# Spreading the sample's cross-attention scores over more of the prompt's work, and giving its projections two banks

## The chip, the cores and the metric

The kernel runs on one core of one Trainium2 chip. The metric is the device time of one execution in microseconds (us). Before the change three runs took 1911.37, 1909.26 and 1916.39 us; their median is 1911.37 us. Five engines work side by side: TensorE (PE, matrix products; its weight loads are listed apart as PEld), VectorE (DVE), ScalarE (ACT), GpSimd (POOL, here mostly an issuer of transfers) and SyncE (SP, an issuer of transfers). Each takes its own instructions strictly in their order, and waits on semaphores for the others.

## The reference

One step of a small decoder with a single layer. It is computed for two groups that share all weights: a prompt of 1024 tokens, and a "sample" of 8 sequences that each add one token to a memory of 8192 cached tokens. Width is 1024, all arithmetic float32.

```python
xp = xp + merge_heads(fox_prompt(q, k, v, logf), sgu_prompt(u, z, ...), ..., w_o)
xp = xp + cross_attend(rmsnorm(xp, g_cross), mk, mv, w_cq, w_co)
xp = xp + conv_ffn(rmsnorm(xp, g_ffn), 0, w_up, conv_w, conv_b, w_down)

att = fox_sample(q, k, v, logf, cache_k, cache_v, cache_logf, page_table)
xs = xs + merge_heads(att, sgu_sample(u, z, ...), ..., w_o)
xs = xs + cross_attend(rmsnorm(xs, g_cross), cache_mem_k, cache_mem_v, w_cq, w_co)
xs = xs + conv_ffn(rmsnorm(xs, g_ffn), state_conv, w_up, conv_w, conv_b, w_down)

def cross_attend(xn, mk, mv, w_cq, w_co):
    q = (xn @ w_cq).reshape(B, T, MEM_HEADS, MEM_HEAD_DIM)
    s = jnp.einsum('bqhd,bmhd->bhqm', q, mk) * (MEM_HEAD_DIM ** -0.5)
    p = jax.nn.softmax(s, axis=-1)
    o = jnp.einsum('bhqm,bmhd->bqhd', p, mv).reshape(B, T, MEM_HEADS * MEM_HEAD_DIM)
    return o @ w_co
```

The change touches the sample's line with `cross_attend` and the projection by `w_o` ahead of it. Here T is 1, there are 4 heads of 256, and each of the 8 sequences has its own cached memory of 256 tokens (1 MB of keys and 1 MB of values each). After both groups are through, each is normalised once more and written out.

## The kernel before

**Two streams of work.** The prompt is written as one Python generator, `prompt()`: projections, attention and the rest in two halves of 512 tokens (`hf` 0 and 1). The sample is another, `sample()`: first the attention over the paged memory (`decode`), then `sample_rest`, which holds everything from the merge of heads to the final output. Both emit instructions into one program. The loop at the end of `build` runs the prompt's generator; each of its yields names an estimate of the microseconds just emitted, which is added to `acc`. Whenever `acc` has reached `PACE` of the running phase (2.9 for `sample_rest`), one step of the sample's generator is drawn and `PACE` taken off:

```python
while bgs and not held[0] and most and acc[0] >= PACE[phase[1] or phase[0]]:
    most -= 1
    acc[0] -= PACE[phase[1] or phase[0]]
    if next(bgs[0], None) is None:
        bgs.pop()
```

So the number of yields in a piece of the sample's code sets how densely it is mixed into the prompt. A scheduler with a model of the engines' times then settles the order of the instructions on each engine; `behind(e)` (L1249) tells it to place what is emitted under it after the newest instruction of the prompt on engine e. The order that counts is therefore that of the built program. In the stretch in question the prompt is in the feed-forward part (`ffn`, L1159) of its second half.

**The prompt's feed-forward.** 22 pairs of columns of `w_up` are taken in groups of 6, 6, 5 and 5. For each of a group's pairs there are two "up" tiles. A tile loads 512 KB of `w_up` by SyncE (L223), splits it into a rounded part on ACT (L209, `wh`) and a remainder on DVE (L210, `wl`), and runs 24 matmuls (L246 to L248) into one bank of PSUM. The bank is read by ACT (L1192, L1193) and then by two DVE operations of the convolution (L1194, L1195); a small one, L1197, mends the first two columns. Per pair follow a SiLU on ACT (L1200), a product on DVE (L1201) and a split into two `u` buffers (ACT L209, DVE L210). After a group's up tiles come its "down" tiles: two halves of columns, each with splits of `w_down` (L209, L210), four row tiles of matmuls, and an addition on DVE (L1226). The prompt's banks are four `ba` and two `bb`; a tile cannot start before its bank's last reader is done. Raw weights have 4 buffers, `wh` 5, `wl` 4.

**The sample's part.** It has two banks of its own, `ms` and `dv`, four buffers `kv` of 1 MB and five `d2` buffers. `sample_proj` multiplies the 8 rows by a 1024x1024 weight (`w_o`, `w_cq` and `w_co` in turn): for each half n of the columns it loads two `kv` buffers by POOL (L1474), runs 8 matmuls (L258) into bank `ms`, copies the bank to a `d2` buffer on ACT (L1462), and folds the four partial sums by one more matmul, again into `ms` (L1465). The second half's matmuls cannot start before the first half's fold has been read. For `w_cq` the result is scaled on DVE (L1520) and written to memory, `q2s_d`, by SyncE (L1521).

The scores follow (L1526 to L1537). For each of the 8 sequences POOL loads the two halves of its query, spread over all partitions (L1529, two `d2` buffers), and its 1 MB of cached keys (L1531, one `kv` buffer); DVE multiplies (L1535, two products of 128x1024) and sums over each head's 256 columns (L1536, one reduce of 128x2048). One yield follows each sequence. Then come the transposes (L1541), a softmax, the cached values (L1564, L1568), the `w_co` projection and the sample's own feed-forward (L1610 to L1653).

Of the kernel before, what the change touches and what calls it, by code (L numbers as in the profile page):

```python
# [12 lines left out]
ALU = mybir.AluOpType  # L13
AX = mybir.AxisListType
PSUM = bass.MemoryType.PSUM
ENG = mybir.EngineType
DRAM = bass.MemoryType.DRAM

P = 128
# [10 lines left out]
FF = 2816  # L30
NF = FF // P
NPAGE = 64
EPS = 1e-6
NEG = -1e30
UW = 1024
# [40 lines left out]
PACE = {'p1': 7.0, 'att0': 20.0, 'mid0': 8.0, 'ffn0': 8.5, 'att1': 15.0, 'mid1': 6.8, 'ffn1': 2.5, 'rest': 2.9}  # L76


def build(nc, tc, ctx, a, phases=None):
# [13 lines left out]
    def nm(s):  # L93
        cnt[0] += 1
        return f"{s}_{cnt[0]}"
# [13 lines left out]
    def KV():  # L109
        return dpool.tile([P, 2048], F32, tag="kv", bufs=NKV, name=nm("kv"))  # L110

    def sm(shape, tag, bufs=2, dt=F32):
        return small.tile(shape, dt, tag=tag, bufs=bufs, name=nm(tag))
# [4 lines left out]
    def BB():  # L118
        return psum.tile([P, 512], F32, tag="bb", bufs=2 + MB, name=nm("bb"))
# [9 lines left out]
    def MS():  # L129
        return BB() if MB else psum.tile([P, 512], F32, tag="ms", bufs=1, name=nm("ms"))  # L130

    def DV():
        return psum.tile([P, 512], F32, tag="dv", bufs=1, name=nm("dv"))

    def D2(n=512, dt=F32):
        return dpool.tile([P, 512], dt, tag="d2", bufs=5, name=nm("d2"))[:, :n]
# [25 lines left out]
    epsb = const.tile([P, 1], F32, tag="epsb", name="epsb")  # L162
    nc.vector.memset(epsb, EPS)
    warm = const.tile([P, 1], F32, tag="warm", name="warm")
# [28 lines left out]
    def rstd_of(ssq, n, width, tag):  # L193

        p = ssq.shape[0]
        r = sm([P, width], tag + "r", 2)[:p]
        nc.vector.tensor_scalar(r, ssq, 1.0 / n, EPS, op0=ALU.mult, op1=ALU.add)
        nc.gpsimd.tensor_tensor(r, r, mhalf[:p, :width], op=ALU.pow)
# [54 lines left out]
    def sample_mm(ps, raw, kk, xT, n, off=0):  # L253

        for q in range(2):
            k = kk * 2 + q
            j = k % 4
            mmul(  # L258
                ps[32 * j : 32 * j + 32, :n],
                xT[:, k, :],  # L260
                raw[:, q, off : off + n],
                start=(k < 4),
                stop=(k >= 4),
                tile_position=(0, 32 * j),
            )
# [43 lines left out]
    def p1(early):  # L309
# [25 lines left out]
        def stats(hf):  # L335
# [9 lines left out]
            for dst, m in ((rstd8, 64.0), (rstd, 1.0)):  # L345
                v = sm([P, 4], "xv", 2)
                nc.vector.tensor_scalar(v, ssx[:, c], m / D, m * EPS, op0=ALU.mult, op1=ALU.add)
                nc.gpsimd.tensor_tensor(dst[:, c], v, mhalf[:, :4], op=ALU.pow)
# [898 lines left out]
    bgs, acc, phase = [], [0.0], ["p1", None]  # L1247

    def behind(e):  # L1249

        return tc.issue_after(last[e]) if e in last else nullcontext()
# [208 lines left out]
    def sample_out(n, ps, fin):  # L1460
        t = D2()
        nc.scalar.activation(t, ps, AF.Copy)  # L1462
        yield 1
        ps2 = MS()
        mmul(ps2[:8, :], selS, t, start=True, stop=True)  # L1465
        fin(n, ps2[:8, :])

    def sample_proj(w, xT, fin):
        for n in range(2):
            ps = MS()  # L1470
            for kk in range(4):
                if kk % 2 == 0:
                    raw = KV().rearrange("p (k n) -> p k n", n=512)
                    nc.gpsimd.dma_start(raw, w[kk * 256 : (kk + 2) * 256, n * 512 : (n + 1) * 512].rearrange("(k p) n -> p k n", p=P))  # L1474
                    yield 1
                sample_mm(ps, raw[:, (kk % 2) * 2 : (kk % 2) * 2 + 2, :], kk, xT, 512)
            yield from sample_out(n, ps, fin)

    def sample_rest(xs):
        yield 1  # L1480
# [31 lines left out]
        def add(n, ps):  # L1512
            nc.vector.tensor_tensor(xs[n], ps, xs[n], op=ALU.add)

        yield from sample_proj(a["w_o"], xsT, add)
        yield from sample_norm(xs, gp[:, G_CROSS : G_CROSS + 8], xsT)
        q2s = pair("s")

        def toq(n, ps):
            nc.vector.tensor_scalar(q2s[n], ps, 1.0 / 16, None, op0=ALU.mult)  # L1520
            nc.sync.dma_start(q2s_d[:, n * 512 : (n + 1) * 512], q2s[n])  # L1521

        yield from sample_proj(a["w_cq"], xsT, toq)

        sS = sm([P, 2, 8, 4], "sS", 1)
        for b in range(8):  # L1526
            qb = [D2(), D2()]
            for n in range(2):
                nc.gpsimd.dma_start(qb[n], q2s_d[b : b + 1, n * 512 : (n + 1) * 512].broadcast_to((P, 512)))  # L1529
            kv = KV()  # L1530
            nc.gpsimd.dma_start(kv.rearrange("p (a c) -> p a c", c=D), a["cmk"][b].rearrange("(a p) c -> p a c", p=P))  # L1531
            kvv = kv.rearrange("p (a c) -> p a c", c=D)
            for n in range(2):
                kn = kvv[:, :, n * 512 : (n + 1) * 512]
                nc.vector.tensor_tensor(kn, kn, qb[n].unsqueeze(1).broadcast_to((P, 2, 512)), op=ALU.mult)  # L1535
            nc.vector.tensor_reduce(sS[:, :, b, :], kv.rearrange("p (a h d) -> p a h d", a=2, h=4), axis=AX.X, op=ALU.add)  # L1536
            yield 1  # L1537
        yield 1
        tr = MS()
        for mt in range(2):  # L1540
# [21 lines left out]
        for b in range(8):  # L1562
            kv = KV().rearrange("p (a c) -> p a c", c=D)
# [11 lines left out]
            op=ALU.mult,  # L1575
# [3 lines left out]
        for n in range(2):  # L1579
            ps = MS()  # L1580
# [3 lines left out]
        sample_T(y, ones[:, 0:8], xsT)  # L1584
        yield 1
        yield from sample_proj(a["w_co"], xsT, add)
        yield from sample_norm(xs, gp[:, G_FFN : G_FFN + 8], xsT)

# [14 lines left out]
        for f4 in range(11):  # L1603
            ps = DV()
# [60 lines left out]
        for n in range(2):  # L1665
            ps = (DV, MS)[n]()
# [89 lines left out]
    def sample():  # L1756
        yield from decode()
        phase[1] = "rest"
        yield from sample_rest(pair("dec"))
# [4 lines left out]
    for t in prompt():  # L1764
        ins = nc.cur_bb.bb.instructions
        for e in (ENG.DVE, ENG.PE):
            for i in range(len(ins) - 1, max(seen, len(ins) - 400) - 1, -1):
                if ins[i].engine == e:
                    last[e] = ins[i]
                    break  # L1770
        acc[0] += t
        most = int(t / PACE[phase[1] or phase[0]]) + 1
        while bgs and not held[0] and most and acc[0] >= PACE[phase[1] or phase[0]]:
            most -= 1
            acc[0] -= PACE[phase[1] or phase[0]]
            if next(bgs[0], None) is None:
                bgs.pop()
        seen = len(nc.cur_bb.bb.instructions)
    for _ in bgs.pop() if bgs else ():
        pass  # L1780
# [90 lines left out]
```

## Time and profile before

| what | value |
|---|---|
| median of three runs | 1911.37 us |
| the profiled execution | 1913.18 us |
| its span, first to last instruction | 1911.4 us |
| mean granted TensorE clock | 0.978 |
| PE busy | 1816.1 us, 95% |
| DVE busy | 1404.6 us, 73% |
| ACT, POOL busy | 761.7 us (40%), 480.6 us (25%) |
| score products L1535 | 16, 1216 ns each, from 1583.8 to 1636.3 us |
| score reduces L1536 | 8, 2274 ns each, from 1593.3 to 1643.4 us |

The profile is one execution. A page gives the busy time of each engine, the chain of work that ended last, and the costliest groups of instructions by line and shape; `ba<-wh,u` reads "written bank, then what was read". Further views of the same trace give the waits of an engine (who waited, for what, how often and how long), windows (the busy time of every engine in a stretch, the granted clock, the DMA engines' share and rate), and the timeline, where each line is one instruction with its start, its length and, in brackets, the idle time ahead of it and what ended that. Matmuls overlap: an instruction is listed as 0.39 us long, but a new one starts every 0.23 us while the clock is full. "Start to start" below is that second kind of time.

### The profile page before, as it was taken

Reading aid. Unit: us, or ns where it says so; the run is one execution under the profiler, and the core shown is the slowest. Engines: PE = TensorE matmul, PEld = TensorE weight load, DVE = VectorE, ACT = ScalarE, POOL = GpSimd, SP = SyncE. Lnnn points to the kernel's source line nnn. Section 1 sums busy time; section 2 is a strip of 40 time slices with the busy share of each in tenths; the row PEclk is TensorE's granted clock in tenths of the full one; section 3 lists DMA queues with packets and bytes.
Section 4 is the critical chain, followed back from the end, with each engine's and each line's share of the span. In section 5 each row is a group of like instructions: output and inputs, shape, how many; then the busy total and the mean of one; then the engine's idle time right before and its main releaser. Section 6 shows DMA issues by size and latency. Waiting matters only on the chain.

```text
span 1911.4 us, 24216 instructions
## 1 busy us (share of the span) xinstructions
PE 1816.1 (95%) x9255; PEld 1296.3 (68%) x9255; DVE 1404.6 (73%) x1662; ACT 761.7 (40%) x1435; POOL 480.6 (25%) x429
## 2 busy tenths in 40 slices
PE   8999999778898999999999999998999999899998
PEld 5987666555676667777777776775665667667765
DVE  4888678777777887989989998887864548754344
ACT  5332356566633435333333244324353333232232
POOL 1232342222121332213432322354222012101110
PEclk9999999989998999999999999998999999899999
DMA  8777988743395876759878879888859557676872
GB/s 322 286 245 278 323 319 302 265 162 119 128 399 210 324 268 256 297 206 359 313 264 313 301 304 344 340 338 302 307 206 362 191 200 265 215 242 247 320 280 101
DMA packets 156373, 517.07 MB, mean 271 GB/s; under 512 B 20169, under 2 KB 41929, under 8 KB 123489
## 3 DMA queue, kind: packets, MB, share of 16 engines
q0 software_dynamic: 56400, 339.04, 47.7%
q1 hardware_dynamic: 92944, 163.89, 24.7%
q10 hardware_dynamic: 6912, 12.59, 1.7%
q8 instruction: 73, 1.20, 0.2%
q14 instruction: 44, 0.35, 0.1%
HBM read 493.63 MB, written 21.84 MB: 270 GB/s over the span
## 4 chain that ended last, share of the span: by engine, by line
PE 66%; DVE 8%; ACT 3%; DMA 3%; issue 2%; POOL 0%; SPq 0%; DVEq 0%; POOLq 0%; ACTq 0%
PE ba L247 9%; PE ba L246 9%; PE ba L248 9%; PE bb L246 6%; PE bb L247 5%; PE bb L248 5%; PE dv L1371 5%; DMA kv<-cache_k,kidx 2%; DVE kv L1312 1%; DVE s L1316 1%; PE dv L1614 1%; PE ba L973 1%; PE ba L975 1%; PE ba L974 1%; PE bb L772 1%
## 5 line engine op out<-in xcount | busy, mean ns | idle before, releaser
L209 ACT ACTIVATE wh<-wr 128x1024 fp32r<-128x1024 f32 (+2 forms) x220 | 228.8, 1044 | 488.8 <-PE ba L247 147.8
L210 DVE TENSOR_TENSOR wl<-wr,wh 128x1024 fp32r<-128x1024 f32 (+2 forms) x220 | 262.5, 1200 | 166.7 <-PE ba L248 71.3
L1306 POOL DMA_INDIRECT kv<-cache_k,kidx x128 | 179.8, 1405 | 545.6 <-DVE s L1316 249.3
L1312 DVE TENSOR_TENSOR kv<-kv,d 128x2048 f32<-128x2048 f32 (+1 forms) x139 | 292.3, 2113 | 28.2 <-DMA kv<-cache_k,kidx 26.9
L1316 DVE TENSOR_REDUCE s<-kv 128x32 f32<-128x2048 f32 (+1 forms) x139 | 292.0, 2106 | 0.6
L1365 POOL DMA_INDIRECT kv<-cache_v,kidx x128 | 181.3, 1416 | 424.2 <-PE dv L1371 169.6
L246 PE MATMUL ba<-wh,u 128*128 128x512 f32 (+1 forms) x596 | 226.9, 382 | 0.0
L247 PE MATMUL ba<-wl,u 128*128 128x512 f32 (+1 forms) x596 | 226.2, 380 | 0.0
L248 PE MATMUL ba<-wh,u 128*128 128x512 f32 (+1 forms) x596 | 223.4, 380 | 1.0 <-DVE u L210 1.0
L246 PE MATMUL ba<-u,wh 128*128 128x512 f32 (+2 forms) x520 | 203.0, 391 | 1.3 <-DVE u L213 1.2
L247 PE MATMUL ba<-u,wh 128*128 128x512 f32 (+2 forms) x520 | 203.8, 392 | 0.0
L248 PE MATMUL ba<-u,wl 128*128 128x512 f32 (+2 forms) x520 | 202.7, 390 | 0.0
L1371 PE MATMUL dv<-kv,s 128*32 128x512 f32 x1024 | 138.0, 618 | 6.8 <-DMA kv<-cache_v,kidx 6.8
L246 PE MATMUL bb<-u,wh 128*128 128x512 f32 (+2 forms) x344 | 138.2, 402 | 1.8 <-DVE u L213 1.8
L247 PE MATMUL bb<-u,wh 128*128 128x512 f32 (+2 forms) x344 | 136.5, 397 | 2.5 <-DVE u L213 2.5
L248 PE MATMUL bb<-u,wl 128*128 128x512 f32 (+2 forms) x344 | 135.9, 396 | 0.0
L246 PEld LDWEIGHTS ba<-wh,u 128*128 128x128 f32 x596 | 112.7, 189 | 31.4 <-issue 8.0
L248 PEld LDWEIGHTS ba<-wh,u 128*128 128x128 f32 x596 | 112.1, 189 | 29.0 <-issue 6.3
L247 PEld LDWEIGHTS ba<-wl,u 128*128 128x128 f32 x596 | 112.4, 189 | 23.8 <-issue 2.9
L247 PEld LDWEIGHTS ba<-u,wh 128*128 128x128 f32 x520 | 98.7, 190 | 33.3 <-issue 13.0
L246 PEld LDWEIGHTS ba<-u,wh 128*128 128x128 f32 x520 | 98.5, 190 | 31.7 <-issue 7.1
L248 PEld LDWEIGHTS ba<-u,wl 128*128 128x128 f32 x520 | 98.5, 189 | 28.5 <-issue 9.3
(418 smaller groups left out, 3105.5 us busy)
## 6 DMA issues: line engine op xcount, KB each, us to landing
wr<-w_up SPq DMA_DIRECT2D x88, 512.0 KB
kv<-w_up POOLq DMA_DIRECT2D x22, 1024.0 KB
wr<-w_down SPq DMA_DIRECT2D x40, 512.0 KB
kv<-w_down POOLq DMA_DIRECT2D x11, 1024.0 KB
wr<-w_in SPq DMA_DIRECT2D x16, 512.0 KB
wr<-w_o SPq DMA_DIRECT2D x16, 512.0 KB
wr<-w_cq SPq DMA_DIRECT2D x16, 512.0 KB
wr<-w_co SPq DMA_DIRECT2D x16, 512.0 KB
```

Source lines behind the costliest of these rows:

```text
L209: nc.scalar.activation(h, src, AF.Copy)
L210: nc.vector.tensor_tensor(l, src, h.bitcast(F32), op=ALU.subtract)
L246: mmul(out, sh, mh, start=(i == 0), stop=False)
L247: mmul(out, sh, ml, start=False, stop=False)
L248: mmul(out, sl, mh, start=False, stop=(i == n - 1))
L772: mmul(po[64 * j : 64 * j + 64, q0:256], vn[:, kt, 64 * j : 64 * j + 64], pt[j][kt // 4][:, kt % 4, q0:256], start=(kt == 0), stop=(kt == ...
L973: mmul(pss[i], mh[k][:, tb], wh, start=(k == korder[0]), stop=False)
L1306: nc.gpsimd.indirect_dma_start(kv, None, a["cache_k"], off(kidx[:, b, ch : ch + 1]))
L1312: nc.vector.tensor_tensor(kvv[:, i : i + m, :], kvv[:, i : i + m, :], qb.unsqueeze(1).broadcast_to((P, m, 512)), op=ALU.mult)
L1316: nc.vector.tensor_reduce(s[:, ch * 4 + i : ch * 4 + i + m, :].rearrange("p k h -> p (k h)"), kvv[:, i : i + m, :].rearrange("p k (h d) -> ...
L1365: nc.gpsimd.indirect_dma_start(kv, None, a["cache_v"], off(kidx[:, b, ch : ch + 1]))
L1371: mmul(dv[32 * j : 32 * j + 32, :], s[:, ch * 4 : ch * 4 + 4, :].rearrange("p k h -> p (k h)"), kvv[:, j, :], start=(ch == 0), stop=(ch == ...
```

## The change

Three things are edited.

1. In the score loop each sequence now yields `CMK` = 3 instead of 1, and the driving loop takes w times `PACE` from `acc` for a step that yields w. A sequence's scores thus use up three steps of the prompt's time instead of one.
2. The score operations are emitted under `behind(ENG.DVE)`, and the one reduce of 128x2048 becomes two of 128x1024. DVE has 8 instructions more in all.
3. In `sample_proj` the first half's sums and fold go to bank `dv`, the second's to `ms`. Both halves' matmuls are issued before either fold. A projection has 5 yields instead of 6.

PE, ACT, POOL and SP issue as many instructions as before.

```diff
+CMK = 3
@@ sample_out
-        ps2 = MS()
+        ps2 = (DV, MS)[n]()
         mmul(ps2[:8, :], selS, t, start=True, stop=True)
         fin(n, ps2[:8, :])
@@ sample_proj
+        outs = []
         for n in range(2):
-            ps = MS()
+            ps = (DV, MS)[n]()
             for kk in range(4):
                 if kk % 2 == 0:
                     raw = KV().rearrange("p (k n) -> p k n", n=512)
                     nc.gpsimd.dma_start(raw, w[...])
                     yield 1
                 sample_mm(ps, raw[:, (kk % 2) * 2 : (kk % 2) * 2 + 2, :], kk, xT, 512)
-            yield from sample_out(n, ps, fin)
+            outs.append(sample_out(n, ps, fin))
+            next(outs[n])
+        for o in outs:
+            yield from o
+        yield 1
@@ sample_rest, for b in range(8)
-            for n in range(2):
-                kn = kvv[:, :, n * 512 : (n + 1) * 512]
-                nc.vector.tensor_tensor(kn, kn, qb[n]..., op=ALU.mult)
-            nc.vector.tensor_reduce(sS[:, :, b, :], kv.rearrange("p (a h d) -> p a h d", a=2, h=4), axis=AX.X, op=ALU.add)
-            yield 1
+            with behind(ENG.DVE):
+                for n in range(2):
+                    kn = kvv[:, :, n * 512 : (n + 1) * 512]
+                    nc.vector.tensor_tensor(kn, kn, qb[n]..., op=ALU.mult)
+                for i in range(2):
+                    nc.vector.tensor_reduce(sS[:, i, b, :], kvv[:, i, :].rearrange("p (h d) -> p h d", h=4), axis=AX.X, op=ALU.add)
+            yield CMK
@@ the driving loop
-            if next(bgs[0], None) is None:
+            w = next(bgs[0], None)
+            if w is None:
                 bgs.pop()
+            else:
+                acc[0] -= (w - 1) * PACE[phase[1] or phase[0]]
```

## The prediction

> **What bounds the kernel now.** I read the page first, then the waits of TensorE, then windows of 20 us, then single instructions.
>
> ```profile
> PE 1816.1 (95%) x9255; PEld 1296.3 (68%) x9255; DVE 1404.6 (73%) x1662; ACT 761.7 (40%) x1435; POOL 480.6 (25%) x429
> PE 66%; DVE 8%; ACT 3%; DMA 3%; issue 2%; POOL 0%; SPq 0%; DVEq 0%; POOLq 0%; ACTq 0%
> ```
>
> TensorE (PE) is the bound, so a change is worth what it adds to or takes from PE's own stream or its idle time. Up to about 1521 us both programs issue the same instructions in the same order on every engine; the first that differs is the sample's w_o block. In the 390 us behind it PE waits twice, and the windows (columns: PE, PE weight loads, DVE, ACT, POOL busy; then the granted clock) show where:
>
> ```profile
> PE bb L246 <- DVE t L1197: 8.0, 1, 8.0
> PE ba L248 <- DVE u L210: 1.0, 1, 1.0
> ...
> 1540.00:1560.00 20.00, 20.00 (x98) 13.90 (x96) 12.36 (x19) 9.29 (x13) 1.06 (x2) 1.00 0.54 200
> 1560.00:1580.00 20.00, 20.00 (x92) 13.12 (x89) 9.92 (x15) 8.35 (x14) 2.95 (x5) 1.00 0.70 247
> 1580.00:1600.00 20.00, 20.00 (x88) 16.35 (x88) 13.76 (x16) 6.00 (x10) 4.99 (x9) 1.00 0.67 193
> 1600.00:1620.00 20.00, 20.00 (x89) 16.26 (x88) 20.00 (x21) 7.36 (x13) 5.42 (x9) 1.00 0.84 303
> 1620.00:1640.00 20.00, 12.01 (x42) 8.97 (x40) 20.00 (x22) 3.92 (x5) 1.99 (x3) 0.74 0.67 230
> ```
>
> VectorE (DVE) is full from 1592 to 1648 us, half empty before. The timeline (start, length, instruction, idle before) shows PE without a bank:
>
> ```profile
> 1621.61 0.40 PE L248 MATMUL ba<-wh,u 128*128 128x512 f32 x1
> 1630.00 0.77 PE L246 MATMUL bb<-wh,u 128*128 128x512 f32 x1 [7.99 <-DVE t L1197]
> 1630.57 0.63 PE L247 MATMUL bb<-wl,u 128*128 128x512 f32 x1
> ```
>
> and, on DVE, why: the bank's last reader, L1195 at 1629.12, stood behind score work.
>
> ```profile
> 1620.59 2.35 DVE L1535 TENSOR_TENSOR kv<-kv,d 128x1024 f32<-128x1024 f32 x2
> 1622.86 2.28 DVE L1536 TENSOR_REDUCE sS<-kv 128x8 f32<-128x2048 f32 x1
> 1625.06 1.21 DVE L210 TENSOR_TENSOR wl<-wr,wh 128x1024 fp32r<-128x1024 f32 x1
> 1626.19 1.22 DVE L1535 TENSOR_TENSOR kv<-kv,d 128x1024 f32<-128x1024 f32 x1
> 1629.12 0.73 DVE L1195 SCALAR_TENSOR_TENSOR t<-bb,gp,t 128x510 f32<-128x510 f32 x1
> ```
>
> From start to start PE loses 8.39 - 0.23 = 8.2 us (its step is 0.23). The clock row is 0.5 from 1624.46 to 1634.70, so the 11 matmuls from 1630.00 step by 0.43: 11 x 0.20 = 2.2 us. A wait at 1641.09 costs 1.1 (step 1.38), smaller ones 0.5. Together 12.0 us, what the scores cost PE today.
>
> **The change part by part.** *Score work.* Per sample row b: two products and a reduce. Start to start a product takes 1.13 us (two in 2.27, above), the reduce 2.20. Split in two it costs two reduces of half size; L1316 has that shape, 1207 ns long, 1.13 start to start, so 2.26. Eight rows: 8 x (2.27 + 2.26) = 36.2 us against 35.8. The added 0.4 us lies on DVE, not on PE.
>
> *Where it goes.* Before, the scores start on DVE at 1583.8 and share eight up tiles. After, the projections end earlier (next part) and the rows come every 3 x 2.9 / 5.2 = 1.7 tiles (yields times PACE, over a tile's own estimate) instead of every 0.6. In the changed DVE order the first product stands behind the first read of up tile 2 of 12, and 12 products and 12 half reduces stand ahead of the L1195 that came late. I sum the order from the first product to that L1195: 12 x 1.13 + 12 x 1.13 (scores) + 9 x 1.13 (weight splits, L210) + 8 x 0.66 (L1194) + 8 x 0.66 (L1195) + 8 x 0.07 (L1197) + 3 x 0.60 (L1201) + 2 x 0.61 (split of u) = 51.4 us.
>
> *When it starts (T1).* By matmul counts, w_cq's block runs at 1544 to 1547.8 and its folds end at 1551.2 and 1554.6. SyncE writes q2s at 1555.4. Before, the second write went out at 1580.99, its load was issued at 1585.42 and DVE started at 1589.47: 8.5 us. So T1 is 1564 at best. At worst the load queues behind the four cmk loads (4 MB), now issued ahead of it on POOL's queue: before, the first q2s load, behind 2 MB, took from 1574.68 to 1583.67, 9.1 us; doubled, 18 us, T1 = 1578. But the 4 MB go out at 1546 to 1549, 11 us or more ahead of the load (before it was 1.6 us), and this queue alone moves about 1 MB in 2.5 us from 3 us after the issue (the DMA view's best slices stand at 399 GB/s), so they are in at 1560 to 1563. I take T1 = 1565.
>
> *What it does to PE.* 1565 + 51.4 = 1616.4 against 1620.5, when PE needs that bank: the 8.2 and 2.2 us go. Late next are the splits of u and the copies for the first down tiles: the same sum carried on gives 1628.9 against 1628.5 and 1630 against 1629.5. The last reduce ends at 1634 to 1637 (before 1645.7). I charge 0.5 to 1.5 us here, take 1.0, and each us of T1 beyond 1565 costs one more. The gain cannot exceed the 12.0.
>
> By the Trainium skill, page "TensorE: Matmul & The Clock Gate", Part 1 on the HAM clock gate, the clock halves after one idle window of about 3.4 us. The trace agrees, with a halved clock in an 8.0 us wait; by that rule a rest under 3.4 us costs only itself, so the sum stays; without it the row's 2.2 per 8.2 us would make 1.0 into 1.3.
>
> *Two banks.* Three projections each trade two blocks of 8 sample matmuls for one of 16. Eight cost PE 2.04 us of its stream (1520.81 to 1523.31 less one step), the block of 16 at L1568 3.76: 2 x 2.04 - 3.76 = 0.3 us, three times 0.9. Folds stay six. The price: the block needs both halves of the weights. w_cq's four loads now all go out at 1522.5 to 1525.3 (buffers come free with w_o's single block) and at 2.5 us per MB plus 3 are in by 1538, needed at 1544. w_co's have 30 us more. Lower bound 0, upper bound 5 us each; taken 0, since the queue's row fits.
>
> *Queues.* SyncE: both q2s writes move ahead of the w_up loads of tiles 9 on. The first load behind them went out at 1557.4 before, the second write now at 1555.4: nothing lost. POOL: cmk loads wait for w_cq's block, not each for a half; same order otherwise. The product held behind the prompt's last DVE instruction (`behind`) waits with prompt reads behind it: L1195 of tile 2, then the weight splits. That is covered while T1 stays near 1565. ACT's copies keep 2.3 us and more to the fold (before 5.0); a copy takes 0.60.
>
> Sum: -12.0 + 1.0 - 0.9 = -11.9. The profiled execution took 1913.2 us (span 1911.4, 1.8 around it), 1.8 above the median of 1911.4. 1913.2 - 11.9 = 1901.3, or 1899.5 against the median; I say 1900.5.
>
> **Rivals.** *B, the backlog only shrinks.* T1 at 1568 to 1573, or the boundary to the down tiles stalls by as much for another reason: a rest of 4 to 9 us, plus 2.2 of half clock, 1904 to 1911. For it: at the boundary my sum leaves nothing over. Against: at 1616 there are 4 us, and T1 has its own 2 us of margin behind the four cmk loads.
>
> *C, slower: DVE's head blocks.* If q2s lands late, the first product holds L1195 and the splits behind it. The loss is T1's lateness plus 1.0, plus 2.2 of half clock. From about 10 us late (T1 1575) that is more than the 12.0 and the 0.9 saved now; 19 us late (T1 1584, where the first product stood before) it is 22.2, 10 us more than now: 1921. For it: DVE already waited for q2s three times:
>
> ```profile
>   DMA d<-q2s_d: 6.2, 3
> ```
>
> Against: the 4 MB lead by 11 us. The Trainium skill, page "DMA: Bandwidth & Descriptors", section "Queues, rings and completion order", says, of the queues that SyncE and ScalarE issue on, that each DMA engine consumes descriptors in ring order; if POOL's queue is alike, small loads pass nothing. That speaks against this change; the 9.1 us behind 2 MB agree. Worked from those rows alone, the whole 4 MB unmoved at the issue gives T1 1578, a loss of 16.2 and 1915: the near end of C, which needs another 6 us.
>
> *D, PE waits in the merged blocks,* for loads or for the copy before a fold: 1 to 6 us, 1901 to 1907.
>
> *E, nothing moves.* The transposes that end the scores stand at the same place of PE's order, two matmuls apart; were the first product to start at 1580 again at the old density, the 12.0 would stay: 1910 to 1912. The changed order speaks against it.
>
> **How the numbers follow.** Forecast 0.62 (1897 to 1903), B 0.14 (0.02 of it far worse than its range), D 0.10, C 0.12 (1915 and more, 0.09 of it beyond 1921), E 0.02. The forecast is the likeliest, so 1900.5. The range leaves out C, E and 0.05 of thin tails: 1896 to 1911. A measurement tells about 0.5%, 9.6 us, from no change: faster means below 1901.8. Of the forecast 0.56 and of D 0.04 lie there: 0.60. Slower, beyond 1921, takes 0.09 of C and those 0.02 of B: 0.11. The rest is 0.29.
>
> **What would show it.** Right: no PE wait over 3 us after 1521, clock 1.0 through 1640, the first score product near 1565 and the last reduce before 1638; DVE at 15 to 18 of 20 us from 1560 to 1620; three blocks of 16 sample matmuls without a gap. Wrong: DVE idle before the first product with a q2s load as what ends it (C, or B), a PE wait on L209 or L210 at the first down tiles (B), on a kv load or L1462 at the blocks (D), or a stall like today's at the same bank (E).

## The result, and the profile after

The changed kernel takes 1902.57 us (median of 20 runs, 1896.12 to 1912.05) against 1911.33 us (20 runs) before: the ratio is 0.9952, with a 95% interval from 0.9942 to 0.9962. That is 9.2 us less by the ratio, a little under the 9.6 us that I had called tellable, though with 20 runs each the interval lies clear of 1; 1900.5 was forecast. The profiled execution took 1900.45 us, its span 1898.7 us.

The waits of TensorE behind the w_o block, and the same windows as before (PE, PE weight loads, DVE, ACT, POOL; then the granted clock). In the changed file the lines up to the projections stand one further down, the scores are L1542 and L1544:

```profile
PE ms L284 <- DVE s L1456: 1.1, 1, 1.1
```

```profile
1540.00:1560.00 20.00, 20.00 (x98) 12.21 (x98) 8.41 (x10) 8.46 (x11) 5.18 (x9) 1.00 0.91 333
1560.00:1580.00 20.00, 20.00 (x88) 16.30 (x87) 19.55 (x23) 6.87 (x13) 5.09 (x9) 1.00 0.83 248
1580.00:1600.00 20.00, 20.00 (x88) 16.32 (x88) 20.00 (x25) 8.31 (x14) 3.79 (x7) 1.00 0.90 304
1600.00:1620.00 20.00, 20.00 (x89) 16.30 (x88) 20.00 (x28) 7.56 (x13) 1.86 (x3) 1.00 0.66 222
1620.00:1640.00 20.00, 20.00 (x89) 15.69 (x88) 17.32 (x25) 6.72 (x9) 1.43 (x2) 1.00 0.57 187
```

PE is busy through all five windows and its clock is full: the 8.0 us wait and the halved clock are gone. DVE is full from 1561 instead of from 1592 us, and has slack again from 1630. Its timeline at the start of the scores (start, length, instruction) shows no idle time ahead of the first product, and prompt work between the products:

```profile
1560.38 0.75 DVE L1195 SCALAR_TENSOR_TENSOR t<-ba,gp,t 128x511 f32<-128x511 f32 x1 [0.36 <-ACT hlast L1194]
1561.18 1.23 DVE L1542 TENSOR_TENSOR kv<-kv,d 128x1024 f32<-128x1024 f32 x1
1562.32 0.74 DVE L1196 SCALAR_TENSOR_TENSOR t<-ba,gp,t 128x510 f32<-128x510 f32 x1
1562.98 0.15 DVE L1198 TENSOR_TENSOR t<-t,fix 128x2 f32<-128x2 f32 x1
1563.17 0.69 DVE L1202 TENSOR_TENSOR t<-t,t 128x512 f32<-128x512 f32 x1
1563.78 1.22 DVE L1542 TENSOR_TENSOR kv<-kv,d 128x1024 f32<-128x1024 f32 x1
```

Two executions differ by some 3 us before either program reaches the change: the last prompt matmul ahead of the w_o block starts at 1520.81 us before and at 1517.70 after, in the same order of work. So I measure each profile from the start of the first matmul of that w_o block (L258 of before) to the start of PE's last instruction, and call it the stretch. Before it is 382.7 us, after 372.8: 9.9 less. A second profile of the changed kernel (below) has 370.9.

Of the 12.0 us lost before, none is left up to the end of the scores. But 2.8 us have come up later, at a place that I had not looked at. The first two lines are PE's timeline, the others POOL's; in brackets is the idle time ahead and what ended it:

```profile
1715.10 0.81 PE L284 MATMUL ms<-cp,s 8*128 8x8 f32 x8 [1.10 <-DVE s L1456]
1716.90 0.63 PE L249 MATMUL ba<-u,wl 128*128 128x512 f32 x1
```

```profile
1696.44 1.57 POOL L1618 DMA_DIRECT2D kv<-w_up  x2 [0.16 <-issue]
1713.25 0.72 POOL L1618 DMA_DIRECT2D kv<-w_up  x1 [15.23 <-DMA o_s<-kv]
1713.99 0.55 POOL L199 TENSOR_TENSOR r1r<-r1r,mhalf 8x1 f32<-8x1 f32 x1
```

The transposes of the sample's third norm (L284) wait for the normalised row, that for the power that makes the norm (L199, on POOL), and that stands in POOL's queue behind a load of the sample's w_up. The load waits 15.2 us for its buffer, which a store of the convolution's state (`o_s1`, in 5632 pieces of 8 numbers) still reads. That store was issued at 1697.3 and had company: from 1702 to 1706 us only 376 packets of under 512 bytes went through while POOL's queue moved 1.62 MB (the loads ahead), from 1706 to 1710, with 0.42 MB left to move, 5184. From start to start PE loses 1.25 us there, and then eight matmuls at 0.43 instead of 0.23, 1.5 us. Before, the same four w_up loads stood in the same order on POOL, but three of them could not go out before w_co's second block:

```profile
1711.31 0.70 POOL L1610 DMA_DIRECT2D kv<-w_up  x1 [25.68 <-PE ms L258]
1724.06 2.28 POOL L1610 DMA_DIRECT2D kv<-w_up  x3 [12.04 <-PE ms L258]
1733.84 0.55 POOL L198 TENSOR_TENSOR r1r<-r1r,mhalf 8x1 f32<-8x1 f32 x1 [7.50 <-DVE r1r L197]
```

There the store (issued at 1713.2) lay beside that wait, with one load ahead of it instead of three: 5018 small packets went from 1717 to 1721. No load waited for it, and the power waited for its own input only. So the earlier loads met the store and, by these counts, also made it slower; no run separates the two.

### The profile page after: what moved, and what is told of

Same layout as the page of the kernel before. It is cut to its first block, busy times and chain, and to the rows that moved or that the text cites. A ratio compares the mean times of both kernels' runs of the same rounds, so it can differ in the third digit from the quotient of the medians.

```text
span 1898.7 us, 24235 instructions
## 1 busy us (share of the span) xinstructions
PE 1810.4 (95%) x9255; PEld 1295.8 (68%) x9255; DVE 1404.6 (74%) x1670; ACT 760.9 (40%) x1435; POOL 475.4 (25%) x429
## 4 chain that ended last, share of the span: by engine, by line
PE 83%; DVE 6%; ACT 4%; DMA 4%; issue 2%; POOL 0%; SPq 0%; DVEq 0%; POOLq 0%; ACTq 0%
PE ba L247 12%; PE ba L248 12%; PE ba L249 12%; PE bb L247 7%; PE bb L248 7%; PE bb L249 7%; PE dv L1372 6%; DVE kv L1313 2%; DMA kv<-cache_k,kidx 2%; DVE s L1317 1%; PE dv L1622 1%; PE ba L974 1%; PE ba L976 1%; PE ba L975 1%; PE ms L773 1%
## 5 line engine op out<-in xcount | busy, mean ns | idle before, releaser
L1307 POOL DMA_INDIRECT kv<-cache_k,kidx x128 | 175.8, 1373 | 552.4 <-DVE s L1317 252.9
```

The costliest lines, as they stand in the source:

```text
L1307: nc.gpsimd.indirect_dma_start(kv, None, a["cache_k"], off(kidx[:, b, ch : ch + 1]))
```

## The experiments

Theory and rivals: the stall went because the scores start earlier (the projections' part), because they are less dense (the scores' part), or only by both. For the new wait: POOL's queue, or the norm's own chain.

**The changed kernel again, either part alone, and the changed kernel with the store out of the way.** These four ran on one chip, in five rounds beside the kernel before (1909.8 us there).

The changed kernel, not edited:

> The changed kernel itself, once more, as the measure for the others beside it. Both theories: 8 to 11 us faster than the kernel before (ratio 0.994 to 0.996), no TensorE wait over 3 us after the w_o block, one wait of about 1 us at the transposes of the sample's third norm (L284) with a stretch of half clock of about 3.4 us behind it.

Measured: 1901.53 us, ratio 0.9958 (0.9945 to 0.9971); the stretch is 370.9 us. The one wait is at L284, 0.7 us, and here the clock stays full behind it, so the half-clock part of the expectation was not met: its 1.5 us stands in one of the two profiles.

The projections alone: `CMK`, `behind`, the halved reduce and the loop's charge are taken back.

```diff
-            with behind(ENG.DVE):
-                ...
-            yield CMK
+            for n in range(2):
+                kn = kvv[:, :, n * 512 : (n + 1) * 512]
+                nc.vector.tensor_tensor(kn, kn, qb[n]..., op=ALU.mult)
+            nc.vector.tensor_reduce(sS[:, :, b, :], ...)
+            yield 1
```

> The two-bank projections alone: the scores keep one yield per sequence, the one reduce of 128x2048, and are not held behind the prompt's DVE work. Theory 'start' (the stall went because the projections end earlier and the first score product moves from 1583.8 to about 1561 us): the 36 us of score work begins 22 us earlier, still as dense as before; the L1195 that came 8 us late has its 46 us of DVE work (1583.8 to 1629.1) start 22 us sooner, so the 8.0 us wait is gone, and the kernel is 8 to 11 us faster, like the whole change (within 3 us of it). Theory 'spacing' (it went because the scores are a third as dense): the wait only moves 22 us forward, at 6 to 8 us with half clock, and the kernel is 0 to 3 us faster.

Measured: 1908.71 us, ratio 0.9997 (0.9985 to 1.0009), stretch 381.7 us. "Start" falls as an explanation of the whole gain. PE's waits:

```profile
PE ms L283 <- DVE s L1455: 2.4, 1, 2.4
PE ms L1546 <- DVE sS L1541: 2.1, 1, 2.1
PE bb L246 <- DVE t L1195: 1.4, 1, 1.4
PE ba L246 <- DVE t L1195: 0.7, 1, 0.7
```

The first score product did start early, at 1563.8. The 8.0 us wait at one bank is gone, but the transposes that end the scores (L1546) now stand 68 matmuls earlier in PE's order, and PE waits for the last reduce and then for a bank whose read that reduce held up:

```profile
1621.45 2.28 DVE L1541 TENSOR_REDUCE sS<-kv 128x8 f32<-128x2048 f32 x1
1623.65 1.22 DVE L210 TENSOR_TENSOR wl<-wr,wh 128x1024 fp32r<-128x1024 f32 x1
1624.78 0.74 DVE L1195 SCALAR_TENSOR_TENSOR t<-bb,gp,t 128x510 f32<-128x510 f32 x1
```

From start to start the three waits at the border of the tiles cost 4.5 us, and 11 matmuls at half clock behind them 2.2: 6.7 are lost there instead of 12.0. Moreover the wait at the norm (L283) costs here 2.6 us, with 1.4 of half clock, 4.0 at a place that lost nothing before. Together PE loses 10.7 us. The time is as "spacing" had it, but the single wait of 6 to 8 us that it named did not come.

The scores' part alone: `sample_out` and `sample_proj` are as before.

```diff
-        ps2 = (DV, MS)[n]()
+        ps2 = MS()
...
-            ps = (DV, MS)[n]()
+            ps = MS()
...
-            outs.append(sample_out(n, ps, fin))
-            next(outs[n])
-        for o in outs:
-            yield from o
-        yield 1
+            yield from sample_out(n, ps, fin)
```

> The score part alone: three yields per sequence, behind the prompt's DVE work, two reduces; the projections as before, one bank and two blocks of 8. Theory 'start': the first product still stands at 1583.8 us, and what lies ahead of each L1195 is hardly less; the TensorE wait stays at 5 to 8 us with half clock, the kernel within 4 us of the one before. Theory 'spacing': the wait is gone or under 2 us, and the kernel is 7 to 10 us faster.

Measured: 1908.99 us, ratio 0.9998 (0.9987 to 1.0009), stretch 381.9 us, as "start" had it. The first product stands at 1582.6, and PE waits as before, for the bank whose last reader is L1196, with the small L1198 right behind it:

```profile
PE bb L247 <- DVE t L1198: 6.1, 1, 6.1
PE ba L248 <- DVE wl L211: 1.0, 1, 1.0
PE ba L247 <- DVE t L1196: 0.4, 1, 0.4
```

Half clock behind it costs another 2.4 us. So the scores' part by itself gains nothing; but this run is no test of rows further apart, because they hardly are. The reduces of the first and of the last sequence stand at

```profile
1593.04 2.34 DVE L1539 TENSOR_REDUCE sS<-kv 128x4 f32<-128x1024 f32 x2
1645.90 2.35 DVE L1539 TENSOR_REDUCE sS<-kv 128x4 f32<-128x1024 f32 x2
```

which is 7.6 us from row to row, against 7.2 before (1593.32 to 1643.42) and 8.7 in the changed kernel (1568.32 to 1628.87). "A third as dense" in the expectations is true of the yields only, nowhere of what DVE runs. Rows set wide apart from the old start were not tried.

The changed kernel with the store out of the way:

```diff
-        nc.sync.dma_start(a["o_s1"], s1)
+        s1c = v8(D2(352))
+        nc.vector.tensor_copy(s1c, s1)
+        nc.sync.dma_start(a["o_s1"], s1c)
```

> The changed kernel, with the convolution state that is written out first copied to a d2 buffer (one DVE copy of 128x352) so that its store, about 16 us long, no longer holds a kv buffer. Theory 'queue' (the new 1.1 us wait at L284 comes from POOL: a w_up load waits 15.2 us for that store, and the power of the norm stands behind it): the w_up load goes out at once, the wait at L284 and the half clock behind it are gone, 2.0 to 3.0 us less than the changed kernel. Rival (the norm's own chain is too long for its place): the wait stays at about 1 us, no change within 1 us.

Measured: 1899.83 us, ratio 0.9951 (0.9938 to 0.9964), stretch 370.1 us, 0.8 less than the changed kernel on the same chip and 2.7 less than its first profile. PE waits nowhere behind the w_o block, and POOL's fourth load goes out 9 us before the power:

```profile
1698.49 0.71 POOL L1620 DMA_DIRECT2D kv<-w_up  x1 [0.91 <-DVE d L1608]
1707.73 0.55 POOL L199 TENSOR_TENSOR r1r<-r1r,mhalf 8x1 f32<-8x1 f32 x1 [8.53 <-DVE t L1198]
```

So the cause of that wait is shown. The medians differ by 1.7 us, less than the 2.0 to 3.0 expected, and the intervals of the two ratios overlap: what it is worth is 0.8 us in an execution without the half clock.

**What in the scores' part does it.** The copied store is kept in the next four, so that the norm's wait does not mix in; the kernel before ran at 1909.48 us beside them. First one yield per sequence, all else as changed:

```diff
-CMK = 3
+CMK = 1
```

> The changed kernel with the copied store, CMK = 1: one yield per sequence, all else kept. Theory 'both' (the earlier start alone leaves about 6.7 us of TensorE loss at the border of the up and down tiles, since the transposes then stand 68 matmuls earlier and the last reduces crowd in front of them; the spacing takes that away): the transposes move to matmul 6240 of the prompt, waits of 3 to 6 us with half clock between 1610 and 1630 us, 5 to 8 us slower than the changed kernel with the copied store (about 1905 to 1908). Rival (the holding behind DVE's prompt work does it, not the yields): no wait over 1 us, 1899 to 1901.

Measured: 1907.10 us, ratio 0.9981 (0.9967 to 0.9996), stretch 377.6 us, 7.5 more than with three yields. PE's waits:

```profile
PE ms L1549 <- DVE sS L1544: 1.8, 2, 1.0
PE bb L247 <- DVE t L1196: 1.5, 1, 1.5
PE ba L247 <- ACT u L210: 0.7, 1, 0.7
PE ba L249 <- DVE u L211: 0.2, 1, 0.2
```

They fall between 1620 and 1625 us, four gaps of 1.1 to 1.8 us from start to start, 4.4 us together, and 2.2 us of half clock follow. Then three yields, without the hold:

```diff
-            with behind(ENG.DVE):
+            with nullcontext():
```

> The changed kernel with the copied store, the score operations not held behind the prompt's newest DVE instruction; CMK stays 3. In the program's order the transposes stand at matmul 6248 instead of 6308. Theory 'both': as with one yield, waits of 3 to 6 us between 1610 and 1635 us, about 1905 to 1908. Rival (the three yields alone spread the scores): no wait over 1 us, 1899 to 1901.

Measured: 1906.50 us, ratio 0.9984 (0.9967 to 1.0002), stretch 377.4 us. The waits are the same kind (1.6 at a bank, 1.0 at the transposes, 0.7 for a split of u, 0.5 at a bank), with 1.3 us of half clock. Without the hold the scheduler closes the scores up again in spite of three yields, to 7.5 us from row to row: the transposes stand at matmul 6248 of the prompt, with the hold and one yield at 6240, with three yields and the hold at 6308.

The reduce left whole:

```diff
-                for i in range(2):
-                    nc.vector.tensor_reduce(sS[:, i, b, :], kvv[:, i, :]..., axis=AX.X, op=ALU.add)
+                nc.vector.tensor_reduce(sS[:, :, b, :], kv..., axis=AX.X, op=ALU.add)
```

> The changed kernel with the copied store and the reduce left whole (one of 128x2048). Order and place of the transposes stay as in the changed kernel. Expected: the score work is 0.4 us less on DVE and PE never waits for it, so the time is the same within 1 us (1899 to 1901). Rival (only halves let the prompt's reads in between): a wait of 1 to 3 us near 1616 to 1630 us, 1901 to 1904.

Measured: 1898.51 us (median of 7 runs, 0.5 below the range named), ratio 0.9941 (0.9916 to 0.9966), stretch 369.7 us, no wait of PE behind the w_o block. Halving the reduce was not needed.

And the projections alone, with the copied store:

> The two-bank projections alone, with the copied store. With the projections alone PE lost 6.7 us at the border of the tiles and 4.0 us (wait 2.6, half clock 1.4) at the sample's third norm. Theory 'queue' (the norm's power stands in POOL's queue behind the load that waits for the store): the 4.0 us go, 1904 to 1906, and the wait at L283 is gone. Rival: under 1 us.

Measured: 1905.98 us, ratio 0.9979 (0.9964 to 0.9993), stretch 375.8 us, 5.9 less than without the copied store; the wait at L283 is gone, 4.0 of it. The others are left, the last one shorter, with five matmuls at half clock behind them instead of 11, which makes most of the rest:

```profile
PE ms L1546 <- DVE sS L1541: 2.1, 1, 2.1
PE bb L246 <- DVE t L1195: 1.4, 1, 1.4
PE ba L246 <- DVE t L1195: 0.2, 1, 0.2
```

With the store out of the way the earlier start alone thus gains 6.9 us of stretch of the 12.6 that both parts gain (4.0 of 9.4 by the ratios); 1.0 of them are the merged blocks.

All stretches side by side, in us. "First product" is counted from the start of the stretch; "row to row" is a seventh of the time from the first sequence's first reduce to the last sequence's:

| kernel | stretch | against before | first product | row to row |
|---|---|---|---|---|
| before | 382.7 | | 62.6 | 7.2 |
| scores' part alone | 381.9 | -0.8 | 62.5 | 7.6 |
| projections alone | 381.7 | -1.0 | 43.2 | 7.2 |
| changed (two profiles) | 372.8, 370.9 | -9.9, -11.8 | 43.2, 43.4 | 8.7, 8.7 |
| changed, copied store | 370.1 | -12.6 | 43.4 | 8.7 |
| ... with one yield | 377.6 | -5.1 | 43.2 | 7.2 |
| ... not held behind DVE | 377.4 | -5.3 | 43.0 | 7.5 |
| ... one reduce | 369.7 | -13.0 | 43.1 | 8.6 |
| projections alone, copied store | 375.8 | -6.9 | 43.1 | 7.2 |

The projections' part starts the scores 19 us earlier. The scores' part, once they start early, sets the rows further apart and so leaves the transposes that end them where they were in PE's order. Only with both does PE lose nothing there.

The version with the copied store is no slower than the changed kernel in any comparison, and its profile loses nothing to waits behind the w_o block. With the reduce whole it has the lowest median seen, 1898.51 us; that ran beside other runs of the kernel before than the changed kernel did, and its interval overlaps that of the changed kernel, so a lead over it is not shown.

## Why the prediction was right, and where it was not

- *The stall and its half clock go.* Right: 12.0 us were lost in this stretch before, nothing after. From the last common matmul to the first additions of the down tiles the changed kernel is 12.6 us shorter (15.7 us at 1654, less the 3.1 that it was ahead at 1521): the 12.0 and two merged blocks. The sum of DVE's order holds too: 51.4 us from the first product to the read of the bank that had come late, 50.9 measured (1561.18 to 1612.03).
- *T1.* Right. 1565 was forecast on the clock of the profile before; the first product started at 1561.2, in an execution that was 3.1 us ahead: 1564.3. The four cmk loads went out at 1543.15 and did not hold the query's loads up; DVE had no idle time for them (0.2 us in the second profile). Rival C, which rested on that, did not come, nor did the order of the queue named there show a cost.
- *The border to the down tiles.* I charged 1.0 us; it cost nothing. Rival B did not come for the whole change. It is what the kernels with only some of the edits show: waits just there, with half clock.
- *Two banks.* Right: 0.9 us forecast for three merged blocks. The w_o block of both halves lies between the prompt matmul at 1517.70 and the second one behind it, at 1521.92. Less two steps of 0.23 that is 3.76 against 2 x 2.04: 0.3 us saved, three times 1.0. (The 2.04 of the prediction is 2.50 less two steps as well, where it says one.) No load and no copy was waited for (rival D).
- *Queues,* the step that failed: "POOL: cmk loads wait for w_cq's block, not each for a half; same order otherwise." The order was the same, but I followed it for w_cq alone. At w_co the merged block frees all four buffers together: the second and third of the sample's w_up loads go out 0.9 us behind the first, not 12.8, and the fourth meets the store of the state, which had lain beside a longer wait until then. It costs 2.8 us in the profile (0.8 in the second). Of these 1.5 are half clock, which I had not charged to a wait as short as 1.1 us.

By these terms the profile's sum is -12.0 - 1.0 + 2.8 = -10.2, measured -9.9; for the second profile -12.0 - 1.0 + 0.8 = -12.2, measured -11.8. Over many runs the kernel gains 9.2 us by the ratio, less than the 11.9 forecast; the norm's wait, which comes in both profiles of the changed kernel and is in no term of mine, has the sign and about the size of what is missing, though how often the half clock follows it was not counted. I had given 0.60 to a time under 1901.8 us; the median, 1902.57, lies just above, in what had 0.29.

Two things helped by luck. The 1.0 us charged at the border and not needed hides part of the norm's wait. And the profiled execution's 1900.45 us, so near to 1900.5, owes 3.1 us to a lead over the profile before that it had when it reached the change.

The sum was right as a whole, yet I had counted the stall's 12.0 us to an earlier start and wider spacing together and only 0.9 to the two banks. The runs show that the two banks, by the earlier start, bring about half of the gain by themselves once the store is out of the way, and that without that their own wait at the norm takes most of it back. The scores' part brings the other half, but only on top of the earlier start; alone it gains nothing that can be told. I had also put the rows at 1.7 tiles apart instead of 0.6, by the yields; DVE ran them 8.7 us apart instead of 7.2. Of the scores' part, the yields and the hold are needed together, the halved reduce not at all.

## What to carry to other kernels

This backlog on a helper engine went only when its work was both started earlier and kept from closing up. The earlier start alone moved the end of the work forward with it, and about half of the loss stayed, one place further on; the edit that was to spread the work spread it only once it started early. So edits should be priced together, and by the place where the work ends as well as where it begins; and how far apart work really runs is read from the engine's order, not from the yields. When a step is moved forward, follow every queue that it feeds at each of its uses, in time and not only in order: a slow store that still reads a buffer, or a small operation behind a load in the same queue, is harmless only as long as something else waits longer. Comparing profiles from the first instruction that differs takes away several microseconds of difference between executions.

## What was not expected of the hardware

PE's clock was halved after waits far shorter than the one before. The Trainium skill, page "TensorE: Matmul & The Clock Gate", Part 1 on the HAM clock gate, puts the halving after an idle window of about 3.4 us, and I had charged short waits by themselves for that. The prediction says that the trace agrees; its own clock row does not: it is 0.5 from 1624.46, 2.45 us after PE's last matmul had ended (1621.61 and 0.40 long). Here a wait of 1.10 us, followed by eight small transposes (0.8 us), was followed by eight matmuls at 0.43 us; one of 2.4 us at the same place by seven (projections alone); waits of 0.7, 1.0, 0.8 and 1.5 us within 7 us by eleven (one yield). A wait of 0.98 us in the kernel before and one of 0.7 us in the second profile of the changed kernel were followed by none. The spells of half clock between the w_o block and PE's last instruction last 3.4, 6.8 or 10.2 us in the clock rows of these profiles. The runs do not tell what besides the length of a wait decides; they show that a wait of 1.1 us cost 2.8 with its half clock, and one of 2.4 us 4.0.
